# Down's first Strassen product on fp16 parts with a scale of its own

## The chip, the cores and the metric

The kernel runs on one core of a Trainium2 chip, as one program. The metric is the device time of one execution in microseconds; a kernel is measured by the median over several runs. Names of engines in this text: TensorE (PE in the profile, its weight loads PEld), VectorE (DVE), ScalarE (ACT), GpSimd (POOL) and SyncE (SP, which here only issues DMAs).

## The reference

An encoder of two layers on one sequence of 1024 tokens with 1024 channels. Each layer mixes tokens by attention and by a convolution module, adds the result to the residual stream x, and then applies a gated feed-forward block, which the change concerns:

```python
for l in range(DEPTH):                      # DEPTH = 2
    h = _rmsnorm(x, g_mix[l])
    ...                                     # attention heads and convolution module
    x = x + y
    h2 = _rmsnorm(x, g_ffn[l])
    z = _dwconv(h2 @ w_up[l], w_dw_ffn[l], b_dw_ffn[l])       # 1024 -> 2 * 2816, kernel of 3
    zg, zv = jnp.split(z, 2, axis=-1)
    x = x + (jax.nn.silu(zg) * zv) @ w_down[l]                # 2816 -> 1024
return _rmsnorm(x, g_final)
```

Everything is float32 in the reference. The kernel has to come close to float32, so it splits each operand of a matmul into a high part and a low part and adds three products: high by high, high by low, low by high.

## The kernel before

A layer runs through projections, attention, the output product with the heads and the convolutions, then Up (`h2 @ w_up`) and Down (the product with `w_down`). The work around the change is laid out by `feed`: a list of steps, each with some matmuls, and for each step a list of other work with a rank. `put(step, rank, f)` files a piece of work, and `feed` walks through the steps, emits the step's matmuls and then the filed work in order of rank. So the order of instructions on each engine is fixed by hand; engines run through their own queues in order and wait for each other by semaphores. All DMAs of this part are issued by SP, except those that add in memory, which POOL issues.

**Up** (`up_steps`). The 2816 channels are 22 blocks f of 128 (NF = 22), for the gate half and the value half. Each block is a 2 by 2 product of halves (tokens, and columns of the weight), made with seven Strassen products i in the order 1, 2, 6, 5, 7, 3, 4 (`UP_ORDER`). One product is one step: 4 tiles of the contraction by 3 part products, 12 matmuls of 128x512. Weights are cast to fp16 parts with a power of two as scale, which comes from the sum of squares of the block's weights: `own_squares` adds them up per partition, `own_total` sums over partitions with a matmul against ones, and `own_scale` makes the exponent from it with small instructions on VectorE. For block f these stand 14 and 12 steps ahead of the block's first product (`UP`), so those of the last block, f = 21, stand in the steps of block 19. `evict` takes products out of PSUM with the scale undone; some products add up in the same bank, and an eviction must come between. After its taps and its gate, a block of activations is squared and added up into a column of `self.ds` (`act_squares`, columns 0 to 21), and so are the rows of `w_down` (`sum_squares`, columns 22 to 43). Activations are stored to memory, except the last four blocks (KEPT = 18), which stay.

**Down** (`down_steps`). The 22 blocks are the contraction. They are cut into two halves of 11, the tokens into two halves of 512 (`done`, `rest`) and the columns of the weight into two halves of 512, and again seven Strassen products are made, in the order 1, 5, 6, 3, 7, 2, 4 (`ORDER`). A step is one product and one channel tile j of 11: four column tiles m by three part products, 12 matmuls. Four PSUM banks hold a product's sum; products 1, 6, 7 and 4 add up in bank set 0, and 5, 3 and 2 in bank set 1 (`BANK_SET`). Before a step of its own, product i needs

- `fetch(i, j)`, 8 steps ahead, even j: two channel tiles of the weight by DMA, into the three buffers `wr`;
- `turn(i, j)`, 4 steps ahead: the weight's parts, into the eight buffers `ws`;
- `combine(i, j)`, 3 steps ahead: the sum or difference of activations;
- `pair(i, j)`, 2 steps ahead: the activations' parts.

Products other than 1 use fp16 parts. Their scales come from all columns of `self.ds`: `total` and `scales` run after step 6 of product 1, since the last activations are only then squared. Product 1 starts before that, and it takes the parts without a scale, in the type fp32r, by the helper `pair` at L1749 (a cast on ScalarE at L1752, a difference on VectorE at L1754). When it is done, `evict(1, m)` adds it to x as it is (L1573), and `rescale(m)` multiplies its bank by the scales of the others, so that product 6 can add to it (L1517). Products of the others are evicted with L1456, their parts made at L1493 and L1494 (weights, two channel tiles at a time) and L1540 and L1541 (activations). The matmuls of all are at L1551, those of Up at L1306; `total` is at L1500, `own_total` at L1246.

In attention, `sums` writes the reciprocals of the softmax sums of a head into a tile `rs`, and a DMA stores that tile to memory (L1904 to L1906).

Of the kernel before, what the change touches and what calls it, by code (L numbers as in the profile page):

```python
# [9 lines left out]
F32 = mybir.dt.float32  # L10
F32R = mybir.dt.float32r
I32 = mybir.dt.int32
F16 = mybir.dt.float16
BF16 = mybir.dt.bfloat16
AF = mybir.ActivationFunctionType
ALU = mybir.AluOpType
AX = mybir.AxisListType
# [15 lines left out]
NF = DFF // 128  # L33
# [65 lines left out]
LEFT = 4  # L99
# [22 lines left out]
BANK_SET = {1: 0, 6: 0, 7: 0, 4: 0, 5: 1, 3: 1, 2: 1}  # L122
# [22 lines left out]
class Encoder:  # L145
# [787 lines left out]
    def scales(self, l, f):  # L933
        nc = self.nc
        ps = self.bank(f"sc{l}p", (128, 9))
        nc.tensor.matmul(ps, self.ones, f[:, 0:9], start=True, stop=True)
        col = lambda i: f[:, i:i + 1]
        nc.vector.tensor_copy(out=f[:, 0:9], in_=ps)
        nc.vector.tensor_tensor(out=col(13), in0=col(0), in1=col(1), op=ALU.add)
        self.half_exponent(col(17), col(13))  # L940
        self.power(col(21), col(17), -1.0, 200.0)
        self.power(col(22), col(17), 1.0, 39.0)
        return col(21), col(22)
# [233 lines left out]
    def up_steps(self, l, steps, put):  # L1177
        nc, a = self.nc, self.a
# [1 line left out]
        seq = START + [(i, f) for f in range(LEFT, NF) for i in UP_ORDER if (i, f) not in START]  # L1180
        base = len(steps)
        at = {p: base + q for q, p in enumerate(seq)}
        self.kept = {}
        raw, wts, zs, st, sums, scale, back, nback = defaultdict(dict), {}, defaultdict(dict), {}, {}, {}, {}, {}
        self.ds = self.cp.tile([128, 2 * NF], F32, name=f"ds{l}", tag="ds", bufs=1)
        sub = lambda o, p, q, op=ALU.subtract: nc.vector.tensor_tensor(out=o, in0=p, in1=q, op=op)
# [27 lines left out]
        def scales(ps, out, w):  # L1214
            ps = ps.rearrange("p (f e) -> p f e", e=2)
            scale, back, nback, v, h = (out[:, i * w:(i + 1) * w] for i in range(5))
            nc.vector.tensor_reduce(out=v, in_=ps, op=ALU.add, axis=AX.X)
            self.half_exponent(h, v)
            self.power(scale, h, -1.0, 204.0)
            for o, at in ((back, self.back), (nback, self.nback)):  # L1220
                nc.vector.tensor_scalar(out=o.bitcast(I32), in0=h.bitcast(I32), scalar1=EXPONENT, scalar2=at, op0=ALU.mult, op1=ALU.add)
            return scale, back, nback
# [19 lines left out]
                squares(f, e, st["sums", f][:, 6:7].bitcast(BF16)[:, e:e + 1])  # L1242

        def own_total(f):
            st["total", f] = self.pp.tile([128, 2], F32, name=f"wt{l}_{f}", tag=f"d{6 + (f > LEFT and (f + 1) % 2)}", bufs=1)
            nc.tensor.matmul(st["total", f], self.ones_b, st["sums", f][:, 6:7].bitcast(BF16), start=True, stop=True)  # L1246

        def own_scale(f):
            scale[f], back[f], nback[f] = scales(st.pop(("total", f)), st.pop(("sums", f)), 1)

        PAIRS = {1: (1, 2), 2: (1, 2), 5: (5, 6), 6: (5, 6), 3: (3, 7), 7: (3, 7), 4: (4,)}

# [141 lines left out]
        for f in range(LEFT):  # L1394
            at_step((13, 13, 15, 15)[f], 6 + f, sum5, f)
            for i, ms in LEFT_AT.items():
                m, g = ms[f], f % 2
# [4 lines left out]
        for q, (i, f) in enumerate(seq):  # L1402
            n = base + q
            steps.append(lambda i=i, f=f: product(i, f))
            m = EVICT.get((i, f), n + 1)
            put(int(m), m % 1 * 10, lambda i=i, f=f: evict(i, f))
        for f in range(LEFT, NF):
            n = m = at[1, f]
# [16 lines left out]
        for f in range(NF):  # L1425
            n = max(at[2, f], at[3, f], at[6, f]) + 1
            n = n if f >= LEFT else TAPS_AT[0][f]
# [4 lines left out]
            m = max(at[7, f], at[4, f]) + 2 if f >= LEFT else TAPS_AT[1][f]  # L1432
# [8 lines left out]
        for j in range(NF // 2):  # L1441
            n = at[1, 7 + j * 13 // 11]
# [7 lines left out]
    def down_steps(self, l, steps, put):  # L1450
        nc, a = self.nc, self.a
        base, last, half = len(steps), l == DEPTH - 1, NF // 2
        done, rest = HALVES
        act, x, casts, w, pairs, ps, nxt, sq, late_r, turns, st = {}, {}, {}, {}, {}, {}, {}, {}, {}, {}, {}
        sub = lambda o, p, q, op=ALU.subtract: nc.vector.tensor_tensor(out=o, in0=p, in1=q, op=op)  # L1455
        plus = lambda o, p, by: nc.vector.scalar_tensor_tensor(out=o, in0=p, scalar=by, in1=o, op0=ALU.mult, op1=ALU.add)  # L1456
# [27 lines left out]

        def turn(i, j):
            raw = casts[i, j - j % 2]
            if i == 1:
                t = self.pair(raw[:, j % 2], f"wd{l}_{i}{j}", "ws")
                w[i, j] = t[:, 0], t[:, 1]
            elif j % 2 == 0:  # L1490
                n = min(2, half - j)
                t = self.tmp("ws", f"wd{l}_{i}{j}", F16, (128, 2, 2, 512))
                nc.scalar.activation(out=t[:, 0:n, 0], in_=raw, func=AF.Copy, scale=st["w"])  # L1493
                nc.vector.scalar_tensor_tensor(out=t[:, 0:n, 1], in0=raw, scalar=st["w"], in1=t[:, 0:n, 0], op0=ALU.mult, op1=ALU.subtract)  # L1494
                for k in range(n):
                    w[i, j + k] = t[:, k, 0], t[:, k, 1]

# [16 lines left out]

        def rescale(m):
            p = ps[BANK_SET[1], m]
            nc.vector.tensor_scalar(out=p, in0=p, scalar1=st["up"], scalar2=None, op0=ALU.mult)  # L1517

        def combine(i, j):
            p, q = act[j], act.get(half + j)  # L1520
# [11 lines left out]
        def pair(i, j):  # L1532
            src = {1: (j, rest), 5: (j, rest), 6: (j, rest), 3: (half + j, done), 7: (j, done), 2: (half + j, rest),
                   4: (half + j, rest)}[i]
            name, tag, raw = f"ab{l}_{i}{j}", "b" if i == 4 else "m", act[src[0]][:, src[1]]
            if i == 1:
                pairs[i, j] = self.pair(raw, name, tag)
            else:
                t = pairs[i, j] = self.tmp(tag, name, F16, (128, 2, 512))
                nc.scalar.activation(out=t[:, 0], in_=raw, func=AF.Copy, scale=st["a"])  # L1540
                nc.vector.scalar_tensor_tensor(out=t[:, 1], in0=raw, scalar=st["a"], in1=t[:, 0], op0=ALU.mult, op1=ALU.subtract)  # L1541
            if i == 4:
                act.pop(half + j)

# [24 lines left out]
        def evict(i, m):  # L1569
            o, cs = {1: (0, rest), 5: (4, done), 6: (0, done), 3: (0, done), 7: (4, done), 2: (0, rest), 4: (4, rest)}[i]  # L1570
            xm = x[o + m][:, cs]
            if i == 1:
                sub(xm, xm, ps[BANK_SET[i], m], ALU.add)  # L1573
            else:
                plus(xm, ps[BANK_SET[i], m], st["nback" if o else "back"])

# [5 lines left out]
        for i, j in order:  # L1582
            n = at[i, j]
# [5 lines left out]
            else:  # L1589
                m = j - tail  # L1590
# [13 lines left out]
        for m in range(4):  # L1604
            put(at[1, half - 1] + 2 + m // 2, 2, lambda m=m: rescale(m))
# [5 lines left out]
        for i in ORDER[:-1]:  # L1611
            for m in range(4):
                put(at[i, half - 1] + 1, 1, lambda i=i, m=m: evict(i, m))
        n5 = at[4, tail]
        for m in range(4):
            if not last:
                put(n5 + m + (m < 3), 1, lambda m=m: evict(4, m))
                continue
            for c in range(2):
                n = n5 + 4 * c + m  # L1620
                put(n + 1 - c, 1 + c, lambda c=c, m=m: evict_end(c, m))
                if m < 3 - c:
                    put(n + 1, 2.5 if c else 2.6, lambda c=c, m=m: gather_end(c, m))
# [8 lines left out]
        sums = lambda c, ks, cs=None: self.norm_sums(l + 1, x, nxt, c, ks, cs)  # L1632
# [148 lines left out]
    def attention(self, l, u, conv, away, spill, kvs, loaded, ahead, wo, begun):  # L1781
        nc = self.nc
# [118 lines left out]
        def sums(h, main, st, y, rb):  # L1901
            pr = self.bank(f"sr{l}_{h}", (8, 128))
            nc.tensor.transpose(pr, st["sums"], self.ident)
            rs = self.cp.tile([8, 128], F32, name=f"rs{l}_{h}", tag="rs", bufs=2)  # L1904
            nc.vector.reciprocal(out=rs, in_=pr)
            nc.sync.dma_start(out=sd[h].rearrange("(a b) -> a b", a=8), in_=rs)  # L1906
            nc.sync.dma_start(out=rb[main, :], in_=sd[h:h + 1].partition_broadcast(64))
            if h == HEADS - 2:
                for c, cs in enumerate(HALVES):
                    agenda[LAST_MULT[c]].append(lambda cs=cs: nc.vector.scalar_tensor_tensor(out=y[main, cs], in0=y[main, cs], scalar=1.0, in1=rb[main, cs], op0=ALU.mult, op1=ALU.mult))  # L1910
            elif h % 2:
                agenda[h * 8 + 10 + Y_DELAY].append(lambda: nc.gpsimd.tensor_tensor(out=y, in0=y, in1=rb, op=ALU.mult))
                agenda[h * 8 + 10 + Y_DELAY + (Y_SPLIT if h < 5 else Y_LAST)].append(
                    lambda: ys.append(self.split(y, f"ys{l}_{h}", on_pool=True)))
# [30 lines left out]
        total = HEADS * 8  # L1945
        agenda = defaultdict(list)
        late, rest = [], {j: list(away[j]) for j in range(4)}
        while any(rest.values()):
            j = max((j for j in rest if rest[j]), key=lambda j: (all(j != e for e, _ in late[-2:]), len(rest[j]), -j))
# [3 lines left out]
        for i, (j, t) in enumerate(late):  # L1953
            n = LATE_FROM + max(int((SIDE_TIME - LATE_FROM) * sum(costs[:i]) / sum(costs)), kinds[i] != "act")
# [31 lines left out]
        for n in range(-2, total + 2):  # L1986
# [13 lines left out]
            if n + 2 < total:  # L2000
                h, qt = divmod(n + 2, 8)
# [202 lines left out]
```

## Time and profile before

| | |
|---|---|
| median of 3 runs | 2181.2 us (2181.03 to 2181.38) |
| profiled execution | span 2179.0 us, 29766 instructions |
| around the span, from the median | 2.2 us |
| busy PE / DVE / ACT / POOL | 2169.7 / 1844.7 / 1456.6 / 537.2 us |
| mean granted clock of TensorE | 0.999 |
| Down's product 1, first layer, by its matmuls' records | 884.85 to 915.25 us |
| the same, second layer | 1965.64 to 1996.05 us |

The span runs from the first to the last instruction of the profiled execution; its time as the runs count it is not listed beside it, so the 2.2 us are the median's excess over this span. Busy time is that in which an engine has an instruction of the program under way. Matmuls overlap, so the duration of one is longer than the distance from one to the next; how fast TensorE goes is read from the distance, that is from many matmuls in a stretch. In the rows of groups, two numbers stand after the count: busy time in us and the mean of one in ns. In the rows by line, three durations in ns are the least, the median and the longest.

### The profile page before, as it was taken

The numbers are of one execution on the slowest core, as the hardware profiler recorded it, in microseconds if no ns is written. First come the engines' busy times: TensorE is split into PE (matmuls) and PEld (weight loads), VectorE is DVE, ScalarE is ACT, GpSimd is POOL, SyncE is SP. The second block draws the span as 40 slices with busy tenths as digits, with TensorE's granted clock in tenths as the row PEclk, the third lists the DMA queues.
The fourth block names the chain that finished last, engine by engine and source line by source line (L and its number), as shares of the span: only waits on it lengthen the run. The fifth ranks groups of instructions, "written<-read, shape, count | busy, mean of one in ns | idle before, by whom it ended". The sixth has DMA issues, their size and how long they took to land.

```text
span 2179.0 us, 29766 instructions
## 1 busy us (share of the span) xinstructions
PE 2169.7 (100%) x10722; PEld 1260.7 (58%) x10722; DVE 1844.7 (85%) x2531; ACT 1456.6 (67%) x2183; POOL 537.2 (25%) x534
## 2 busy tenths in 40 slices
PE   9999999999999999999999999999999999999998
PEld 8887665754444444644488876667544444446445
DVE  6989999879998887887859789998898888878877
ACT  6455888746898886554623668886478888865544
POOL 1223777211111111000012355771112111110000
PEclk9999999999999999999999999999999999999999
DMA  6898878754688885554578986886646888856533
GB/s 195 184 187 212 164 152 171 245 163 104 149 244 259 222 261 145 193 178 151 166 177 164 188 207 134 159 186 200 175 100 164 261 241 242 241 141 218 182 111 122
DMA packets 163013, 400.96 MB, mean 184 GB/s; under 512 B 21888, under 2 KB 29936, under 8 KB 162864
## 3 DMA queue, kind: packets, MB, share of 16 engines
q0 software_dynamic: 62528, 145.89, 36.4%
q1 hardware_dynamic: 100048, 252.63, 33.8%
q8 instruction: 84, 1.38, 0.3%
q10 hardware_dynamic: 288, 0.53, 0.1%
q14 instruction: 65, 0.53, 0.1%
HBM read 270.75 MB, written 69.66 MB: 156 GB/s over the span
## 4 chain that ended last, share of the span: by engine, by line
PE 98%; ACT 1%; DVE 1%; issue 0%; DMA 0%; DVEq 0%; ACTq 0%
PE p L1306 36%; PE pd L1551 18%; PE po L1026 7%; PE s L1818 7%; PE t L1858 5%; PE pq L245 3%; PE pa L245 3%; PE o L1880 2%; PE pkv L245 2%; PE pg L245 2%; PE pg L564 2%; PE pn L245 2%; PE o L1885 1%; PE pv L1794 1%; PE pk L245 1%; PE pa L564 1%
## 5 line engine op out<-in xcount | busy, mean ns | idle before, releaser
L1306 PE MATMUL p<-b,w 128*128 128x512 f16 x3696 | 800.0, 379 | 0.2
L1306 PEld LDWEIGHTS <-w 128*128 128x128 f16 x3696 | 358.7, 98 | 431.9 <-issue 0.8
L1551 PE MATMUL pd<-ab,wd 128*128 128x512 f16 (+2 forms) x1920 | 404.2, 373 | 0.0
L1196 POOL DMA_DIRECT2D wu<-in_w_up x176 | 152.2, 879 | 770.2 <-DVE w L1270 581.5
L1551 PEld LDWEIGHTS <-wd 128*128 128x128 f16 x1656 | 161.9, 98 | 179.4 <-issue 0.5
L1818 PE MATMUL s<-k,q 96*128 96x512 f16 x768 | 186.9, 379 | 0.0
L1270 DVE SCALAR_TENSOR_TENSOR w<-wu,wf,w 128x512 f16<-128x512 f32 (+1 forms) x216 | 177.2, 834 | 3.6 <-ACT w L1267 3.6
L1861 DVE SCALAR_TENSOR_TENSOR pt<-t,pt 128x512 f16<-128x512 f32 x256 | 163.0, 676 | 10.0 <-ACT pt L1860 9.0
L1267 ACT ACTIVATE w<-wu,wf 128x512 f16<-128x512 f32 (+1 forms) x216 | 164.8, 781 | 0.1
L1860 ACT ACTIVATE pt<-t 128x512 f16<-128x512 f32 x256 | 139.1, 596 | 32.0 <-PE t L1858 30.0
L1820 DVE TENSOR_REDUCE mx<-s 128x1 f32<-128x1024 f32 x128 | 155.0, 1211 | 1.0 <-PE s L1818 1.0
L1540 ACT ACTIVATE ab<-ac,ds 128x512 f16<-128x512 f32 x108 | 75.5, 717 | 108.7 <-DVE ac L1455 73.0
L1828 ACT ACTIVATE p<-s,mx 128x1024 f32<-128x1024 f32 x128 | 143.3, 1120 | 2.2 <-DVE mx L1820 1.8
L2039 DVE SCALAR_TENSOR_TENSOR conv<-gate,par,conv 128x1009 f32<-128x1009 f32 (+14 forms) x110 | 139.9, 1274 | 3.1 <-ACT conv L659 0.4
L2056 POOL TENSOR_SCALAR late<-gate,par 128x1019 f32<-128x1019 f32 (+13 forms) x99 | 135.5, 1368 | 27.2 <-PE pn L245 13.9
L1858 PE MATMUL t<-ident,p 128*128 128x128 f32 x1024 | 136.6, 275 | 0.9 <-ACT p L1828 0.6
L1858 PEld LDWEIGHTS t<-ident,p 128*128 128x128 f32 x1024 | 116.8, 141 | 34.8 <-issue 7.4
L1766 DVE SCALAR_TENSOR_TENSOR o<-zg,par,o 128x1023 f32<-128x1023 f32 x88 | 112.7, 1281 | 8.9 <-ACT o L1760 7.4
L1314 DVE SCALAR_TENSOR_TENSOR zg<-p,wf,zg 128x512 f32<-128x512 f32 x72 | 54.0, 750 | 71.2 <-PE p L1306 61.6
L1766 DVE SCALAR_TENSOR_TENSOR v<-zv,par,v 128x1023 f32<-128x1023 f32 x88 | 112.1, 1276 | 0.0
L1818 PEld LDWEIGHTS <-q 96*128 96x128 f16 x768 | 74.0, 97 | 64.6 <-issue 2.1
L1541 DVE SCALAR_TENSOR_TENSOR ab<-ac,ds,ab 128x512 f16<-128x512 f32 x108 | 79.9, 748 | 19.2 <-ACT ab L1540 19.2
(2179 smaller groups left out, 3814.1 us busy)
## 6 DMA issues: line engine op xcount, KB each, us to landing
wu<-in_w_up SPq DMA_DIRECT2D x98, 512.0 KB
wu<-in_w_up POOLq DMA_DIRECT2D x176, 256.0 KB, 4.8
sd<-in_w_down SPq DMA_DIRECT2D x44, 512.0 KB
ws<-sd SPq DMA_DIRECT2D x44, 512.0 KB
act<-v SPq DMA_DIRECT2D x36, 512.0 KB
ac<-act SPq DMA_DIRECT2D x72, 256.0 KB
wo<-in_w_o POOLq DMA_DIRECT2D x32, 256.0 KB, 7.7
x_mix<-y SPq DMA_DIRECT2D x32, 256.0 KB
```

Of the source, the lines that this page charges most:

```text
L245: nc.tensor.matmul(ps[:, HALVES[c]], w, x[:, HALVES[c]], start=(k == 0 and s == 0), stop=(k == n - 1 and s == 2))
L1026: self.nc.tensor.matmul(ps, p[:, sl], q[:, cs], start=(k == 0 and t == 0), stop=(k == 3 and t == 2))
L1196: nc.gpsimd.dma_start(out=dst, in_=src, accum_op=ALU.add)
L1267: nc.scalar.activation(out=t, in_=src, func=AF.Copy, scale=scale[f])
L1270: nc.vector.scalar_tensor_tensor(out=t, in0=src, scalar=scale[f], in1=hi, op0=ALU.mult, op1=ALU.subtract)
L1306: nc.tensor.matmul(ps, w[p][:, k * 128:(k + 1) * 128], b[:, q], start=(i in (1, 5, 2) and k == 0 and t == 0), stop=(k == 3 and t == 2), sk ...
L1551: nc.tensor.matmul(ps[t, m][:, cs], w[i, j][p][:, m * 128:(m + 1) * 128], b[:, q, cs], start=(i in (1, 5, 2) and j == 0 and s == 0), stop= ...
L1766: self.nc.vector.scalar_tensor_tensor(out=o[:, a:b], in0=z[:, at + a:at + b], scalar=self.par[l][:, tap:tap + 1], in1=o[:, a:b], op0=ALU.m ...
L1818: nc.tensor.matmul(ps[:, cs], q[0:96, i, qs], k[0:96, j, cs], start=(s == 0), stop=(s == 2))
L1820: nc.vector.tensor_reduce(out=mx, in_=ps, op=ALU.max, axis=AX.X, negate=True)
L1858: nc.tensor.transpose(tp[:, i, qi * 128:(qi + 1) * 128], st["p"][2 * qp + qi][:, kt * 128:(kt + 1) * 128], self.ident)
L1861: nc.vector.scalar_tensor_tensor(out=lo, in0=tp, scalar=P_SCALE, in1=hi, op0=ALU.mult, op1=ALU.subtract)
```

## The change

Product 1 of Down is made on fp16 parts like the other six. Its scales are ready before Down starts: `own_total` of Up's last block gets a second matmul, which sums those columns of `ds` over partitions that belong to the first half of the channels (activation blocks 0 to 10 and weight rows 0 to 10, 22 columns), and `own_scale` makes from them a scale for the activations, one for the weights and their inverse, in a new small tile `dw`. `turn`, `pair` and `evict` lose their special case for product 1 and use these scales; `rescale` multiplies by the inverse too. So that the new tile has room, `rs` in attention gets one buffer in place of two. The helper `pair` is not called by these functions any more.

```diff
         def own_total(f):
-            st["total", f] = self.pp.tile([128, 2], F32, ...)
-            nc.tensor.matmul(st["total", f], self.ones_b, st["sums", f][:, 6:7].bitcast(BF16), start=True, stop=True)
+            n = 2 + NF * (f == NF - 1)
+            st["total", f] = self.pp.tile([128, n], F32, ...)
+            nc.tensor.matmul(st["total", f][:, 0:2], self.ones_b, st["sums", f][:, 6:7].bitcast(BF16), start=True, stop=True)
+            if f == NF - 1:
+                half = self.ds[:, 0:2 * NF].rearrange("p (e h f) -> p e h f", e=2, h=2)[:, :, 0]
+                nc.tensor.matmul(st["total", f][:, 2:n], self.ones, half, start=True, stop=True)
 
         def own_scale(f):
-            scale[f], back[f], nback[f] = scales(st.pop(("total", f)), st.pop(("sums", f)), 1)
+            ps = st.pop(("total", f))
+            scale[f], back[f], nback[f] = scales(ps[:, 0:2], st.pop(("sums", f)), 1)
+            if f == NF - 1:
+                t = self.cp.tile([128, 8], F32, name=f"dw{l}", tag="dw", bufs=1)
+                nc.vector.tensor_reduce(out=t[:, 0:2], in_=ps[:, 2:2 + NF].rearrange("p (e f) -> p e f", e=2), op=ALU.add, axis=AX.X)
+                nc.vector.tensor_scalar(out=t[:, 0:2], in0=t[:, 0:2], scalar1=2.0 ** -60, scalar2=None, op0=ALU.max)
+                self.half_exponent(t[:, 2:4], t[:, 0:2])
+                self.power(t[:, 4:6], t[:, 2:4], -1.0, 204.0)
+                self.power(t[:, 6:8], t[:, 2:4], 1.0, 50.0)
+                nc.vector.tensor_tensor(out=t[:, 6:7], in0=t[:, 6:7], in1=t[:, 7:8], op=ALU.mult)
+                self.opened.update(a=t[:, 4:5], w=t[:, 5:6], back=t[:, 6:7])
...
         def turn(i, j):
             raw = casts[i, j - j % 2]
-            if i == 1:
-                t = self.pair(raw[:, j % 2], f"wd{l}_{i}{j}", "ws")
-                w[i, j] = t[:, 0], t[:, 1]
-            elif j % 2 == 0:
-                n = min(2, half - j)
+            if j % 2 == 0:
+                n, by = min(2, half - j), self.opened["w"] if i == 1 else st["w"]
                 t = self.tmp("ws", f"wd{l}_{i}{j}", F16, (128, 2, 2, 512))
-                nc.scalar.activation(out=t[:, 0:n, 0], in_=raw, func=AF.Copy, scale=st["w"])
-                nc.vector.scalar_tensor_tensor(out=t[:, 0:n, 1], in0=raw, scalar=st["w"], in1=t[:, 0:n, 0], op0=ALU.mult, op1=ALU.subtract)
+                nc.scalar.activation(out=t[:, 0:n, 0], in_=raw, func=AF.Copy, scale=by)
+                nc.vector.scalar_tensor_tensor(out=t[:, 0:n, 1], in0=raw, scalar=by, in1=t[:, 0:n, 0], op0=ALU.mult, op1=ALU.subtract)
...
         def rescale(m):
             p = ps[BANK_SET[1], m]
-            nc.vector.tensor_scalar(out=p, in0=p, scalar1=st["up"], scalar2=None, op0=ALU.mult)
+            nc.vector.tensor_scalar(out=p, in0=p, scalar1=st["up"], scalar2=self.opened["back"], op0=ALU.mult, op1=ALU.mult)
...
         def pair(i, j):
...
-            if i == 1:
-                pairs[i, j] = self.pair(raw, name, tag)
-            else:
-                t = pairs[i, j] = self.tmp(tag, name, F16, (128, 2, 512))
-                nc.scalar.activation(out=t[:, 0], in_=raw, func=AF.Copy, scale=st["a"])
-                nc.vector.scalar_tensor_tensor(out=t[:, 1], in0=raw, scalar=st["a"], in1=t[:, 0], op0=ALU.mult, op1=ALU.subtract)
+            by = self.opened["a"] if i == 1 else st["a"]
+            t = pairs[i, j] = self.tmp(tag, name, F16, (128, 2, 512))
+            nc.scalar.activation(out=t[:, 0], in_=raw, func=AF.Copy, scale=by)
+            nc.vector.scalar_tensor_tensor(out=t[:, 1], in0=raw, scalar=by, in1=t[:, 0], op0=ALU.mult, op1=ALU.subtract)
...
         def evict(i, m):
...
             if i == 1:
-                sub(xm, xm, ps[BANK_SET[i], m], ALU.add)
+                plus(xm, ps[BANK_SET[i], m], self.opened["back"])
...
         def sums(h, main, st, y, rb):
...
-            rs = self.cp.tile([8, 128], F32, name=f"rs{l}_{h}", tag="rs", bufs=2)
+            rs = self.cp.tile([8, 128], F32, name=f"rs{l}_{h}", tag="rs", bufs=1)
```

More of the change, by code (lines that the diff above doesn't have):

```diff
@@ L1182, in up_steps @@
         at = {p: base + q for q, p in enumerate(seq)}
-        self.kept = {}
+        self.kept, self.opened = {}, {}
         raw, wts, zs, st, sums, scale, back, nback = defaultdict(dict), {}, defaultdict(dict), {}, {}, {}, {}, {}
@@ L1244, in own_total @@
         def own_total(f):
-            st["total", f] = self.pp.tile([128, 2], F32, name=f"wt{l}_{f}", tag=f"d{6 + (f > LEFT and (f + 1) % 2)}", bufs=1)
-            nc.tensor.matmul(st["total", f], self.ones_b, st["sums", f][:, 6:7].bitcast(BF16), start=True, stop=True)
-        def own_scale(f):
-            scale[f], back[f], nback[f] = scales(st.pop(("total", f)), st.pop(("sums", f)), 1)
+            n = 2 + NF * (f == NF - 1)
+            st["total", f] = self.pp.tile([128, n], F32, name=f"wt{l}_{f}", tag=f"d{6 + (f > LEFT and (f + 1) % 2)}", bufs=1)
+            nc.tensor.matmul(st["total", f][:, 0:2], self.ones_b, st["sums", f][:, 6:7].bitcast(BF16), start=True, stop=True)
+            if f == NF - 1:
+                half = self.ds[:, 0:2 * NF].rearrange("p (e h f) -> p e h f", e=2, h=2)[:, :, 0]
+                nc.tensor.matmul(st["total", f][:, 2:n], self.ones, half, start=True, stop=True)
+        def own_scale(f):
+            ps = st.pop(("total", f))
[9 more added lines that the diff above has]
+                self.opened.update(a=t[:, 4:5], w=t[:, 5:6], back=t[:, 6:7])
         PAIRS = {1: (1, 2), 2: (1, 2), 5: (5, 6), 6: (5, 6), 3: (3, 7), 7: (3, 7), 4: (4,)}
```

## The prediction

> **What bounds the kernel now.** I read the page first (engines, slices, chain), then the chain of waits in order of time around the two places that the change touches, then the groups by form, and last the timelines of TensorE, VectorE and ScalarE there.
>
> ```profile
> span 2179.0 us, 29766 instructions
> ...
> PE 2169.7 (100%) x10722; PEld 1260.7 (58%) x10722; DVE 1844.7 (85%) x2531; ACT 1456.6 (67%) x2183; POOL 537.2 (25%) x534
> ...
> PEclk9999999999999999999999999999999999999999
> ...
> PE 98%; ACT 1%; DVE 1%; issue 0%; DMA 0%; DVEq 0%; ACTq 0%
> ```
>
> TensorE is busy for 2169.7 of 2179.0 us at full granted clock, and the chain that ended last lies on it for 98%. Only what changes TensorE's own stream, or what makes it wait, can move the end. The chain around the change (start, length, what, how many instructions), in the first layer, and its one row for the second that matters:
>
> ```profile
> 838.55 0.00 PE wt L1246
> 838.56 46.64 PE p L1306 x216
> 885.20 19.06 PE pd L1551 x84
> 904.26 0.15 PE ds0p L1500 x2
> 904.41 158.65 PE pd L1551 x732
> ...
> 1965.99 19.07 PE pd L1551 x84
> ```
>
> The first 84 and the next 48 matmuls of L1551 are Down's product 1 (11 channel tiles, 4 column tiles, 3 part products: 132). They run at 19.06/84 = 226.9 ns each; the last 216 of Up, on fp16 parts with the same 128x512 moving tile, at 46.64/216 = 215.9 ns. No gap stands between the pieces. The rows by form say which is which:
>
> ```profile
> L1551 PE MATMUL pd<-ab,wd 128*128 128x512 f16 x1512 | 327.3, 379 | 0.0
> ...
> L1551 PE MATMUL pd<-ab,wd 128*128 128x512 f32 x264 | 61.1, 392 | 0.0
> ```
>
> 264 = 2 layers of 132. The means (379, 392) are durations of overlapping instructions; the spacing is in the chain.
>
> **The change, part by part.**
>
> *1. Product 1's matmuls become fp16.* At the spacing of Up's row, 84 take 18.14 us where 19.06 stands: 0.92 less. The piece of 732 holds 48 of product 1 and 684 fp16 ones: 732 at 215.9 ns would be 158.06, so the 48 cost 0.59 more than fp16 ones would (at the 11 ns of the 84 it would be 0.53). Together 1.45 to 1.51 us a layer; I take 1.48, for two layers 2.96 us, all of it on the path. Below this nothing comes unless fp16 pieces in this stage run slower than in Up; 684 of them already stand in the same piece.
>
> *2. One more matmul with fp32 ones, 22 columns, behind the last own total of Up (L1246).* It appears as two instructions, as the 44-column ds0p does (0.15 us on the chain). A nearer case is L1228, eight columns of fp32 between fp16 matmuls:
>
> ```profile
> 441.75 0.12 PE wt L1228 x2
> ...
> L1228 PEld LDWEIGHTS wt<-wa,ones_r x4: 190/190/190, 441.4 to 1522.4; 128*128 128x128 f32 x4
> ```
>
> That bounds it below at 0.12. Here it follows the two-column total, whose piece on the chain is 0.00, so it has no long matmul to load its first weights behind; above, I take both loads of 190 ns bare, 0.38. The first load can still begin while the total's predecessor runs out, so I take 0.2 a layer: 0.4 in all. The two ends are 0.24 and 0.76.
>
> *3. Six small VectorE instructions (reduce, maximum, exponent, two powers, product) in the last own scale.* The same six stand in Down's scales:
>
> ```profile
> 904.45 0.20 DVE L1505 TENSOR_REDUCE ds<-ds0p 128x2 f32<-128x44 f32 x1 [4.18 <-PE ds0p L1500]
> 904.69 0.17 DVE L1506 TENSOR_SCALAR ds<-ds 128x2 f32<-128x2 f32 x1
> ...
> 905.38 0.15 DVE L1511 TENSOR_TENSOR ds<-ds 128x1 f32<-128x1 f32 x1
> ...
> 905.64 0.69 DVE L1754 TENSOR_TENSOR ab<-ac,ab 128x512 fp32r<-128x512 f32 x1
> ```
>
> From 904.45 to 905.38 is 0.93 us. Queued behind them on VectorE are filter taps, a weight part and the zv eviction that TensorE's next product on that bank needs:
>
> ```profile
> 843.87 0.75 DVE L1314 SCALAR_TENSOR_TENSOR zv<-p,wf,zv 128x512 f32<-128x512 f32 x1 [0.86 <-PE p L1306]
> ```
>
> VectorE idles 0.86 us before that eviction, so it comes at most 0.07 late; the product that adds on the bank is a whole product away (12 x 0.216 = 2.59 us, less 0.75 for the eviction). Cost: nothing. The matmul of part 2 waits for the squares in ds that it reads; the last of them are written before block 18 starts, and it stands nine steps of 12 matmuls later, so this costs nothing either.
>
> *4. The casts of weights and activations change form.* Rows of the old and of the new form (the new one is already used by the other six products):
>
> ```profile
> L1752 ACT CAST ab<-ac x22: 602/607/621, 879.6 to 1987.2; 128x512 fp32r<-128x512 f32 x22
> L1754 DVE TENSOR_TENSOR ab<-ac,ab x22: 681/686/694, 880.7 to 1989.4; 128x512 fp32r<-128x512 f32 x22
> L1752 ACT CAST wd<-wd_10r x4: 608/609/611, 875.5 to 1958.8; 128x512 fp32r<-128x512 f32 x4
> ...
> L1493 ACT ACTIVATE wd<-wd_52r,ds x2: 1133/1134/1136, 910.7 to 1991.5; 128x1024 f16<-128x1024 f32 x2
> L1494 DVE SCALAR_TENSOR_TENSOR wd<-wd_52r,ds,wd x2: 1278/1280/1281, 912.1 to 1992.9; 128x1024 f16<-128x1024 f32 x2
> ...
> L1540 ACT ACTIVATE ab<-ac,ds x108: 704/721/725, 910.0 to 2138.4; 128x512 f16<-128x512 f32 x108
> L1541 DVE SCALAR_TENSOR_TENSOR ab<-ac,ds,ab x108: 741/747/755, 910.8 to 2149.0; 128x512 f16<-128x512 f32 x108
> ...
> L1456 DVE SCALAR_TENSOR_TENSOR x<-pd,ds,x x52: 473/743/752, 943.3 to 2169.5; 128x512 f32<-128x512 f32 x44, 128x256 f32<-128x256 f32 x8
> L1455 DVE TENSOR_TENSOR x<-x,pd x8: 681/684/686, 914.5 to 1997.1; 128x512 f32<-128x512 f32 x8
> L1517 DVE TENSOR_SCALAR pd<-pd,ds x8: 754/758/761, 919.4 to 2003.4; 128x512 f32<-128x512 f32 x8
> ```
>
> Activations: 11 x (721 - 607) = 1.25 us more ScalarE and 11 x 61 ns = 0.67 us more VectorE a layer. Weights: eleven pairs of about 0.61 and 0.69 become five of 1.13 and 1.28 and one single (0.71, 0.75): ScalarE 6.7 to 6.4, VectorE 7.5 to 7.15. Eviction of product 1 becomes the form of the others (L1455 0.684 to L1456 0.743, four a layer, 0.24 us), and the rescale keeps its operation and gets a second scalar (L1517, 0.758 now; bounds 0 and 0.06, as for the evictions, four a layer). VectorE's sum in the stage grows by about 0.6 us. Whether TensorE sees that depends on three margins.
>
> *Opening.* Both halves of a weight pair are now cast at the even step, one step early for the odd one.
>
> ```profile
> 883.43 1.24 ACT L1760 ACTIVATE o<-zg,par 128x1024 f32<-128x1024 f32 x1 [2.66 <-DVE zg L1314]
> ...
> 885.22 0.69 DVE L1754 TENSOR_TENSOR ab<-ac,ab 128x512 fp32r<-128x512 f32 x1 [1.82 <-ACT ab L1752]
> ```
>
> Activation tile 1 is ready at 885.91; TensorE starts on it at 885.20 + 12 x 0.216 = 887.79 after the change. The cast is 0.11 + 0.06 longer, and the weight pair ahead of it adds up to 0.6 on VectorE, of which the idle times shown (2.66, 1.82) take most. At worst 886.7: 1.1 us to spare. Tiles 2 to 7 have more.
>
> *Around Down's total.* VectorE waits 4.18 us for ds0p, then makes tile 8 of the activations, ready at 905.64 + 0.69 = 906.33. TensorE starts it 12 matmuls after 904.41: 907.13 before; after the change 907.00, against 906.39. It uses the low part in its second matmul: 0.8 us of cover, the thinnest of all. With that gone, each 0.1 us late costs 0.1 us a layer.
>
> *After product 1.* TensorE comes 0.5 us earlier from the total on:
>
> ```profile
> 920.69 0.75 DVE L1541 SCALAR_TENSOR_TENSOR ab<-ac,ds,ab 128x512 f16<-128x512 f32 x1
> ```
>
> This is tile 3 of product 5, ready at 921.44. TensorE uses it at 904.41 + 48 x 0.228 + 36 x 0.216 = 923.13, after the change 922.55; VectorE's surplus since the total is 4 x 0.06 for casts and 0.24 for evictions, at most 0.12 for rescales, so 922.0: 0.5 us left, and the low part is not needed until one matmul later. No wait.
>
> *5. The queues and buffers.* SP's fetch of a later weight pair waits for VectorE to have read an older one; that read now ends one step sooner, so loads are issued up to 2.6 us earlier, at a DMA share of 0.46 in the first part of this stage:
>
> ```profile
> SPq L1482 <- DVE wd L1754: 43.7, 12, 6.1
> ...
> 884.85:904.10 19.25, 19.25 (x87) 15.93 (x86) 14.53 (x19) 12.57 (x22) 0.00 (x0) 1.00 0.46 146
> ```
>
> POOL issues nothing here. Six slots of the weight buffer are taken in place of eleven, so slot waits can only shrink. In attention the reciprocal tile rs has one buffer in place of two: a head's reciprocal waits for the store of the head before.
>
> ```profile
> L1905 DVE RECIPROCAL rs<-sr x14: 931/933/935, 245.2 to 1454.2; 8x128 f32<-8x128 f32 x14
> ...
> SPq L1907 <- DMA sd<-rs: 30.8, 14, 3.8
> ...
> 361.75 0.94 DVE L1905 RECIPROCAL rs<-sr 8x128 f32<-8x128 f32 x1
> ...
> 373.40 0.94 DVE L1905 RECIPROCAL rs<-sr 8x128 f32<-8x128 f32 x1
> ```
>
> The store lands within 3.8 us, while the closest two stand 11.6 us apart (361.75 and 373.40). Cost: nothing.
>
> *Sum.* -2.96 + 0.4 = -2.56 us against the profiled span of 2179.0, that is 2176.4. The median of the runs is 2181.2, 2.2 us more than this span, for what lies around it: 2178.6. With the ends of parts 1 and 2: 2178.2 to 2179.1.
>
> **A rule weighed against the rows.** The weight load takes 190 ns for fp32 and 98 for fp16:
>
> ```profile
> L1551 PEld LDWEIGHTS <-wd x1656: 95/98/181, 915.2 to 2169.1; 128*128 128x128 f16 x184
> L1551 PEld LDWEIGHTS pd<-ab,wd x264: 187/188/192, 884.8 to 1995.6; 128*128 128x128 f32 x132
> ```
>
> If that load were in the open, 264 x 90 ns = 23.8 us would go and the time would be 2157.8. The spacing differs by 11 ns only, so it is hidden behind the matmul before. The Trainium skill, "TensorE: Matmul & The Clock Gate", section "Weight-path perf modes — Fast Weight Load (FWL) and DoubleRow", says that 128 non-fp32 weights load about twice as fast and fp32 gains nothing; the two rows agree. The same page's "Back-to-back issue gap" gives 512/2.4 + 2.5 = 215.8 ns a matmul with no term for the type: the fp16 rows agree; the 226.9 does not, and by that rule the saving would be zero.
>
> **The rivals.**
> - *Nothing is saved* (0.06): the 227 ns come from this stage (its banks, its reads) and not from the type. For it: the 48 behind the total are not quite as the 84. Against: 684 fp16 matmuls into the same banks at 215.9. Time: 2181.2 + 0.4 = 2181.6.
> - *The other side: TensorE waits for VectorE in the opening* (0.07). In-order double casts of 1.28 us stand ahead of the activation casts. It begins to cost once tile 1 is more than 1.9 us late (887.79 less 885.91), and the kernel is slower than before once it is 1.9 + 1.28 = 3.2 us late, twice. Two more double casts and an eviction ahead of it (1.28 + 1.28 + 0.75 = 3.3) would do that: 2181.4; a third cast gives 2183.9, and 0.2% slower needs 5.4 us. Against: the idle times above.
> - *A thin margin fails by a little* (0.10): tile 8 or product 5's tile 3 comes up to 1 us late; up to 2 us are given back: 2178.6 to 2180.6.
> - *The weight load is in the open* (0.02): 2157.8.
> - *My forecast* (0.75): 2178.6.
>
> **How the numbers follow.** A measurement of this kernel tells about 0.2% from no change, 4.4 us: 2176.8 to 2185.6. The forecast lies within it, as do the first and third rivals and most of the second. The range for 8 in 10 takes in the forecast and the third rival, with half a microsecond below for a spacing better than Up's: 2177.6 to 2180.8. Faster by over 0.2% gets 0.05 (open load, and a forecast wrong by two thirds), slower 0.04, the same 0.91.
>
> **What the changed profile would show.** On the chain 84 matmuls of L1551 at 18.14 us, not 19.06, and no f32 form there; a new piece of 0.1 to 0.4 us behind the last own total; no idle time or stretched spacing at tile 1, tile 8 or product 5; VectorE still idle some 4 us before ds0p. Wrong would be: spacing still 227, a wait of TensorE for an ab tile, or a piece of waiting on the chain in Up's last four blocks.

## The result and the profile after

The changed kernel takes 2178.45 us (median of 21 runs, 2177.97 to 2179.8), the kernel before 2181.38 us in the runs beside it (21 runs, 2180.82 to 2182.24): ratio 0.9986, 95% interval 0.998 to 0.9993. That is 2.93 us less, or 0.13%, where 2.56 was the sum of the prediction.

The page of the changed kernel: span, engines, and the share of engines in the chain that ended last.

```profile
span 2177.3 us, 29765 instructions
...
PE 2167.7 (100%) x10726; PEld 1237.7 (57%) x10726; DVE 1848.6 (85%) x2533; ACT 1459.4 (67%) x2173; POOL 537.1 (25%) x534
...
PE 96%; ACT 1%; DMA 1%; DVE 1%; issue 0%; SPq 0%; DVEq 0%; ACTq 0%
```

All of Down's matmuls of 512 columns are now one form, the 264 that were f32 among them (1512 + 264 = 1776):

```profile
L1560 PE MATMUL pd<-ab,wd 128*128 128x512 f16 x1776 | 384.6, 379 | 0.0
```

TensorE has 2.0 us less of work, VectorE 3.9 and ScalarE 2.8 us more, and TensorE is still what ends the kernel. The chain in order of time (start, length, what, count) around the change, first layer and second; L1247 is the own total, L1250 the new matmul, L1320 Up, L1560 Down, L1511 Down's total:

```profile
839.50 0.00 PE wt L1247
839.50 0.24 PE wt L1250 x2
839.74 46.62 PE p L1320 x216
886.37 18.13 PE pd L1560 x84
904.50 0.15 PE ds0p L1511 x2
904.65 157.99 PE pd L1560 x732
...
1918.91 0.00 PE wt L1247
1918.91 0.24 PE wt L1250 x2
1919.15 46.62 PE p L1320 x216
1965.78 18.13 PE pd L1560 x84
1983.91 0.15 PE ds1p L1511 x2
1984.06 157.99 PE pd L1560 x732
```

A layer's account is read here piece by piece: 19.06 to 18.13 (-0.93), 158.65 to 157.99 (-0.66), the new piece (+0.24), Up's 216 (-0.02): -1.37 us, -2.74 in two layers. A second way, which needs no pieces, is the distance from the last own total of the first layer to that of the second. Before, the second stood here:

```profile
1919.34 0.00 PE wt L1246
```

1919.34 - 838.55 = 1080.79 before, 1918.91 - 839.50 = 1079.41 after: 1.38 us less. The two agree. The profiled span fell by only 1.7 us, since this execution reached the first own total 0.95 us later than the one before (839.50 against 838.55), ahead of everything that the change does in Down. That is the scatter of single executions and not the change: of the kernels below that have the changed code up to there, e6 and e7 have 838.51 and 838.53, e4 and e8 839.19 and 839.22, and e5, with the code of before, has 839.23. In the execution of the changed kernel the chain went through a load:

```profile
11.01 13.51 DMA x<-in_x
```

The chain of the execution of before has no such piece, but a late start does not need one (that of e5 has none either). The distance between the layers is free of it and is used for all kernels below.

### The profile page after: what moved, and what is told of

The parts are those of the page before. It is cut to its first block, busy times and chain, and to the rows that moved or that the text cites. A ratio compares the mean times of both kernels' runs of the same rounds, so it can differ in the third digit from the quotient of the medians.

```text
span 2177.3 us, 29765 instructions
## 1 busy us (share of the span) xinstructions
PE 2167.7 (100%) x10726; PEld 1237.7 (57%) x10726; DVE 1848.6 (85%) x2533; ACT 1459.4 (67%) x2173; POOL 537.1 (25%) x534
## 3 DMA queue, kind: packets, MB, share of 16 engines
q8 instruction: 84, 1.38, 0.3%
## 4 chain that ended last, share of the span: by engine, by line
PE 96%; ACT 1%; DMA 1%; DVE 1%; issue 0%; SPq 0%; DVEq 0%; ACTq 0%
PE p L1320 36%; PE pd L1560 18%; PE po L1026 7%; PE s L1827 7%; PE t L1867 5%; PE pq L245 3%; PE pa L245 3%; PE o L1889 2%; PE pkv L245 2%; PE pg L245 2%; PE pn L245 2%; PE o L1894 1%; PE pv L1803 1%; PE pg L564 1%; PE pk L245 1%; DMA x<-in_x 1%
## 5 line engine op out<-in xcount | busy, mean ns | idle before, releaser
L1320 PE MATMUL p<-b,w 128*128 128x512 f16 x3696 | 800.3, 379 | 0.3
L1320 PEld LDWEIGHTS <-w 128*128 128x128 f16 x3696 | 358.8, 98 | 431.7 <-issue 0.8
L1560 PE MATMUL pd<-ab,wd 128*128 128x512 f16 (+1 forms) x1920 | 400.6, 371 | 0.0
L1560 PEld LDWEIGHTS <-wd 128*128 128x128 f16 x1920 | 187.9, 98 | 209.9
```

The lines of the kernel that those rows point to most:

```text
L1320: nc.tensor.matmul(ps, w[p][:, k * 128:(k + 1) * 128], b[:, q], start=(i in (1, 5, 2) and k == 0 and t == 0), stop=(k == 3 and t == 2), sk ...
L1560: nc.tensor.matmul(ps[t, m][:, cs], w[i, j][p][:, m * 128:(m + 1) * 128], b[:, q, cs], start=(i in (1, 5, 2) and j == 0 and s == 0), stop= ...
```

## The experiments

**e1: the price without the gain.** The functions `own_total` and `own_scale` of the changed kernel, the tile `dw` and the single buffer for `rs`, put into the kernel before; nothing uses the new scales.

```diff
-    nc.tensor.matmul(st["total", f], self.ones_b, ...)
+    nc.tensor.matmul(st["total", f][:, 0:2], self.ones_b, ...)
+    nc.tensor.matmul(st["total", f][:, 2:n], self.ones, half, ...)      # f == NF - 1
+    ...                                                                 # six instructions on VectorE
```

> The kernel before with only the new total added: the 22-column matmul, the six small VectorE instructions, the tile dw and one buffer for rs; product 1 stays on fp32r parts and the new scales are not used. My theory: two instructions of TensorE cost 0.24 us a layer on the chain (as in the changed kernel), the VectorE instructions, the tile and the single buffer cost nothing: 2181.4 + 0.5 = 2181.9 us, product 1 still 19.06 us for 84 matmuls. Rival (VectorE's 0.93 us delays an eviction in Up's last blocks): over 1 us more, above 2182.4, with a piece of waiting on the chain behind block 19.

Measured: 2181.49 us against 2181.3, ratio 1.0002 (0.9992 to 1.0011). The chain:

```profile
838.82 0.00 PE wt L1247
838.83 0.24 PE wt L1250 x2
...
885.69 19.05 PE pd L1565 x84
...
1919.74 0.00 PE wt L1247
```

The piece is 0.24 us as in the changed kernel, and product 1 takes as long as before. TensorE's chain runs on without a wait, so VectorE's six instructions delay nothing. Layer to layer 1080.92, 0.13 more than before, where the pieces (0.24 for the pair, some 0.04 less in the others) give 0.20; to about 0.1 us is what such a distance can tell. The time's interval cannot tell 0.5 us from none.

**e2: the fp32 total ahead of the bf16 one.** In the changed kernel, the two matmuls of `own_total` change places.

> The changed kernel with the 22-column fp32 total ahead of the two-column bf16 total of the same block, not behind it. If the 0.24 us come from the first fp32 weight load that has no long matmul to hide behind, the piece falls to the 0.12 to 0.15 us of the other fp32 pairs, 0.1 us a layer, 2178.2 us. Rival (the pair costs what its 22 columns cost, wherever it stands): 0.24 us stays, 2178.4 us.

```profile
839.00 0.13 PE wt L1249 x2
839.13 0.01 PE wt L1250
...
1918.25 0.13 PE wt L1249 x2
```

0.24 becomes 0.14 with the bf16 total. The columns are the same, so it is the place that counts, and the reading that the first fp32 weight load now hides behind a matmul of 512 columns fits; the rival, that the columns set the price, falls. 2178.18 us (ratio to before 0.9986, 0.9977 to 0.9995), layer to layer 1079.25, which is 0.16 less than the changed kernel.

**e3: one buffer for `rs` in the kernel before.** The edit is `bufs=2` to `bufs=1`, nothing else.

> The kernel before with one buffer for rs in place of two, nothing else. My theory: no wait, 2181.4 us within 0.1%, the reciprocals start 11.6 us apart at the least as before. Rival (the single buffer or the shifted addresses of all later tiles cost or bring time): a difference over 0.3 us between the layers' starts of attention and of its end in the trace.

2181.28 us, ratio 1.0001 (0.9992 to 1.001).

```profile
838.65 0.00 PE wt L1246
...
1919.43 0.00 PE wt L1246
```

Layer to layer 1080.78 against 1080.79. To within the 0.1 us of such a distance, the single buffer costs nothing, and neither do the shifted addresses of the tiles behind it.

**e4: product 2 on fp32r in the changed kernel.** The special case that product 1 lost, given to product 2.

```diff
 def turn(i, j):
+    if i == 2:
+        t = self.pair(raw[:, j % 2], f"wd{l}_{i}{j}", "ws")
+        w[i, j] = t[:, 0], t[:, 1]
...
 def pair(i, j):
+    if i == 2:
+        pairs[i, j] = self.pair(raw, name, tag)
...
 def evict(i, m):
+    if i == 2:
+        sub(xm, xm, ps[BANK_SET[i], m], ALU.add)
```

> The changed kernel with Down's product 2 on fp32r parts without a scale, as product 1 was before; it starts a fresh sum in the other bank set. If the 11 ns a matmul belong to the type, 132 matmuls of product 2 now stand 227 ns apart and the kernel takes 1.48 us more a layer, 2181.4 us. Rival (the 11 ns belonged to the opening of Down, its banks or reads): product 2 stays at 216 ns and the time at 2178.4 us.

2181.28 us, ratio to before 1.0 (0.9991 to 1.0009): the gain is gone.

```profile
839.19 0.00 PE wt L1247
...
886.05 18.13 PE pd L1566 x84
904.18 0.15 PE ds0p L1514 x2
904.34 159.47 PE pd L1566 x732
...
1920.08 0.00 PE wt L1247
```

Product 1 keeps its 18.13, and the piece that holds product 2 grows from 157.99 to 159.47: 1.48 us for 132 matmuls, 11.2 ns each, in another place and into the other bank set. Layer to layer 1080.89, 1.48 more than the changed kernel. So the surplus belongs to the type, and the rival that it belonged to this stage falls. The profile of before already spoke against that rival, at a place where the prediction did not look: the projections, far from Down, are on fp32r parts too, and their 48 matmuls of 512 columns take 10.88/48 = 226.7 ns each.

```profile
40.01 10.88 PE pa L245 x48
```

Which operand's type makes the surplus, that of the weights or that of the moving tile, is not told apart by any run here.

**e5 and e10: what the 11 ns consist of.** In the kernel before, each fp32r matmul of product 1 is cut into two of 256 columns (e5) or four of 128 (e10), each with its own weight load.

```diff
-nc.tensor.matmul(ps[t, m][:, cs], w[i, j][p]..., b[:, q, cs], ...)
+for q4 in ((slice(0, 256), slice(256, 512)) if i == 1 else (cs,)):       # e10: four of 128
+    nc.tensor.matmul(ps[t, m][:, q4], w[i, j][p]..., b[:, q, q4], ...)
```

> The kernel before with each fp32r matmul of product 1 cut into two of 256 columns, 264 a layer, each with its own weight load of 188 ns. If the columns set the 227 ns and the load is hidden behind them, a half one takes no less than the load: about 190 ns, 50 us for product 1 in place of 30, 40 us more in two layers (2221 us). Rival (the load with what follows it sets 227 ns whatever the columns): 60 us for product 1, 60 us more (2241 us). Second rival (loads overlap fully, also behind a short matmul): 114 ns, no change of time.

2184.85 us against 2181.39, one time each. My theory (2221 us) was wrong; of the three forecasts the last, called the second rival, was nearly right. The chain of e5 has

```profile
839.23 0.00 PE wt L1246
...
885.87 20.14 PE pd L1552 x168
...
906.16 159.22 PE pd L1552 x780
```

168 in 20.14 us are 119.9 ns each, though one load takes 192 ns. By their records, loads thus overlap one another, and not only the matmul ahead. 226.9 for 512 columns and 119.9 for 256 give 107.0 for 256 columns (0.418 ns a column) and 12.9 left over for each matmul. The fp16 matmuls have the same price a column: 215.9 at 512 and, by the single records at the end of Down, 109.1 at 256 differ by 106.8 (0.417 ns a column), with 2.3 left over. The 11 ns are thus a fixed surplus of an fp32r matmul, as far as two sizes show it.

> The kernel before with each fp32r matmul of product 1 cut into four of 128 columns, 528 a layer. Cut into two, the distance was 120 ns (20.14 us for 168), whole it is 227: a fixed 13 ns beside 0.418 ns a column. My theory (a fixed surplus for each matmul of this type, whatever its columns): 66 to 67 ns, 336 of them in 22.4 us on the chain up to Down's total, about 5 us a layer more than before, 2191 us. Rival (weight loads of 190 ns overlap only two deep): 95 ns, 336 in 31.9 us, 20 us a layer more, 2221 us.

2241.01 us against 2181.27, one time each, and neither my theory's 2191 nor the rival's 2221:

```profile
887.39 37.47 PE pd L1552 x336
...
L1552 PEld LDWEIGHTS pd<-ab,wd 128*128 128x128 f32 x1056 | 118.4, 192 | 0.3
```

37.47/336 = 111.5 ns a matmul of 128 columns, where 66 were forecast. The weight loads follow each other without a gap, one each 111.5 ns. That the columns do not set this distance is shown by the profile of before, where eight fp32 matmuls of one column take 0.89/8 = 111 ns each:

```profile
2170.30 0.89 PE rx_768p L275 x8
```

So the likeliest bound is the load, one for each matmul, which the matmul of 256 columns (119.9) just covers and that of 512 by far. Some other floor of a matmul of this type is not excluded, and the fixed 12.9 ns could not be put to a third size here.

**e6, e7, e8: how thin the cover is.** Idle instructions of VectorE are put at three places of the changed kernel, a maximum of a tile with itself:

```diff
+def idle():
+    k = self.kept[19][:, rest]                       # e8: kept[18]
+    for _ in range(2):                               # e8: 8
+        sub(k, k, k, ALU.max)
+put(base + 6, 2.9, idle)                             # e7: base + 12, 2.5; e8: base - 1, 2.9
```

For e6 and e7 they are two, in a step of product 1 and of product 5; for e8 eight, in the last step of Up. Each has one time. The cover is the start of the second matmul of a tile (the first that uses the low part) less the end of that tile's cast, by the single records.

> The changed kernel with two idle VectorE instructions of 0.61 us each (a maximum of a tile with itself) ahead of the cast of activation tile 8 of product 1, behind Down's scales. In the changed kernel that tile's low part is ready 0.66 us before TensorE uses it. My theory: of 1.22 us, 0.56 come out as a wait of TensorE at tile 8, in each layer: 1.1 us more than the changed kernel, 2179.5 us. Rival (there is more cover than the records show): no stretched distance at tile 8.

2179.79 us. The chain leaves TensorE where it waits and runs through the cast of tile 8:

```profile
906.20 0.75 DVE ab L1550
...
907.00 155.58 PE pd L1560 x719
```

TensorE's distance there is 917 ns where 216 is usual, 0.70 us of wait; two more of 0.13 and 0.12 come at tiles 3 and 4 of product 5. Together 0.95 us a layer (0.85 by the distance from layer to layer), more than the 0.56 expected. An idle instruction takes 0.72 us from start to start and not 0.61; both work on one tile, so that the second seems to wait for the first. And the lateness is carried on to product 5, which I had thought VectorE would make up.

> The changed kernel with the same two idle VectorE instructions behind the first two rescales, ahead of tile 3 of product 5, which has 0.53 us of cover, tile 4 behind it 0.41. My theory: 0.7 us of wait at tile 3 and 0.1 at tile 4, 0.8 us a layer, 2180.1 us. Rival (VectorE catches up): no stretched distance there.

2179.95 us. The distances at tiles 3 and 4 of product 5 are 1063 and 330 ns: 0.85 and 0.11 us of wait, 0.96 a layer (0.92 by the distance from layer to layer) where 0.8 was expected.

> The changed kernel with eight idle VectorE instructions (4.9 us) in the last step of Up, ahead of the cast of activation tile 1 of product 1. VectorE has 1.92 us of idle time there and the tile 1.20 us of cover. My theory: 4.9 - 1.9 - 1.2 = 1.8 us of wait at tile 1, and 0.5 at the tiles behind it at the most, since the queue behind is full: 2 us a layer, 2182.4 us, which would be slower than before. Rival (the opening has more cover): no wait up to 4.9 us, 2178.4 us.

2183.7 us, above the kernel before (2181.39 beside it). VectorE's cast of tile 1 in the changed kernel:

```profile
887.05 0.75 DVE L1550 SCALAR_TENSOR_TENSOR ab<-ac,dw,ab 128x512 f16<-128x512 f32 x1 [1.92 <-ACT ab L1549]
```

The timeline of VectorE in e8, and behind it the chain:

```profile
884.77 5.76 DVE L1469 TENSOR_TENSOR v<-v 128x512 f32<-128x512 f32 x8
890.46 0.74 DVE L1550 SCALAR_TENSOR_TENSOR ab<-ac,dw,ab 128x512 f16<-128x512 f32 x1
...
890.46 0.75 DVE ab L1550
891.21 0.04 issue
891.25 15.48 PE pd L1560 x71
```

The eight take 5.76 us; 5.76 - 1.92 - 1.20 = 2.64, and TensorE's distance at tile 1 is 2739 ns, 2.52 of wait, with none behind it (cover 0.78 and 0.32 at tiles 2 and 3). So the cover read from the records holds to about 0.1 us, and a delay here that is large enough makes the kernel slower than the one before: layer to layer e8 has 1081.91, 1.12 more than before.

**e9: both totals on bf16.** The squares are added up in bf16, and the new total and Down's total become one bf16 matmul each.

```diff
+self.db = self.ds[:, 0:NF].bitcast(BF16)
-nc.scalar.activation(..., func=AF.Square, accum_out=self.ds[:, f:f + 1])
+nc.scalar.activation(..., func=AF.Square, accum_out=self.db[:, f:f + 1])
-nc.tensor.matmul(st["ps"], self.ones, self.ds[:, 0:2 * NF], ...)
+nc.tensor.matmul(st["ps"], self.ones_b, self.db, ...)                    # and own_total's alike
-f = self.ds[:, 0:16]
+f = self.ds[:, NF:NF + 16]
```

> The changed kernel with the sums of squares of activations and of w_down's rows kept in bf16, so that the 22-column total and Down's 44-column total are one bf16 matmul each against bf16 ones, as the own totals of Up. If the fp32 pairs cost 0.24 and 0.15 us a layer on the chain and a bf16 total 0.00 to 0.03, the kernel is 0.7 us faster than the changed one: 2177.8 us. Rival (the small matmul itself is not what costs, but the change of type in the stream): the pieces stay at 0.1 us or more, 2178.2 us.

2177.6 us (2177.32 to 2178.25, 11 runs), ratio to before 0.9984 (0.9975 to 0.9993); the kernel before had 2181.34 beside it.

```profile
839.15 0.00 PE wt L1248
839.15 0.04 PE wt L1251
...
903.95 0.02 PE ds0p L1514
...
1918.17 0.01 PE wt L1248
```

0.24 and 0.15 us become 0.04 and 0.02, and the layer distance 1079.02, 0.39 less than the changed kernel's (0.33 by these two pieces). The rival, that the change of type in the stream costs 0.1 us whatever the matmul, falls. This is the fastest of the kernels by its chain and by its median; by the times alone its interval overlaps that of the changed kernel.

## Why the prediction was right, step by step

**The spacing (part 1)** carried the sum and held: 18.13 us measured for 18.14. The 48 behind the total saved 0.66 where 0.59 was the upper value, so the term is 1.59 us a layer and not 1.48. The 0.07 come from the 732, which now stand 157.99/732 = 215.8 ns apart and not 215.9 as in Up. Why the 48 had cost more than 11 ns each shows in the records of before: right behind the total one distance is 314 ns and most of the next nine are 230 to 236, before they settle at 227. Two sizes off, -3.18 for -2.96 here and +0.48 for +0.4 below, make most of the difference between the 2.56 us predicted and the 2.74 by the chain. The remaining 0.2 to the medians' 2.93 lies well inside the interval of the ratio. e4 shows that the type is the cause. The rival that nothing is saved is out.

That 2178.6 us was forecast and 2178.45 measured is closer than the saving itself, by luck: the three runs it started from lay 0.2 us lower than the 21 beside the result. The lower end of the prediction's sum was added up wrong, too: its own ends give 2179.0 - 3.02 + 0.24 + 2.2 = 2178.4 and not 2178.2.

**The added pair (part 2)** cost 0.24 where 0.2 was taken between 0.12 and 0.38. The reason given fits: e2 takes 0.1 away by putting the pair behind a long matmul. The upper end, two loads bare at 190 ns, was too high: e10 shows fp32 loads each 111.5 ns, and two of these are 0.22.

**VectorE's six instructions (part 3)** took as long as their rows of before (840.87 to 841.83, 0.96 us for 0.93) and cost nothing:

```profile
840.87 0.17 DVE L1257 TENSOR_REDUCE dw<-wt 128x2 f32<-128x22 f32 x1
...
841.83 1.28 DVE L1775 SCALAR_TENSOR_TENSOR v<-zv,par,v 128x1023 f32<-128x1023 f32 x1
...
845.03 0.75 DVE L1328 SCALAR_TENSOR_TENSOR zv<-p,wf,zv 128x512 f32<-128x512 f32 x1
```

The zv eviction comes 5.53 us after the own total, before 843.87 - 838.55 = 5.32; less the 0.24 of the new matmuls it is on time, and its idle time of 0.86 us is used up, as counted.

**The cover (part 4)** was right in that TensorE waits nowhere in this stage, and its sizes were too large. By the records the cover is 1.20 us at tile 1 (predicted 1.1 up to the first matmul, 1.3 up to the second), 0.66 at tile 8 (0.8), 0.53 at tile 3 of product 5 (0.5 up to the first matmul, 0.7 up to the second), and 0.41 at its tile 4, which the prediction did not look at. It called tile 8 the thinnest of all, but it had counted tile 8 up to the second matmul and tile 3 only up to the first; counted alike, tile 3 was already the thinner one. At tile 8 and tile 3 VectorE was ready when the prediction said, to 0.1 us; TensorE came sooner. The prediction took the start of a piece of the chain, here 904.65 us, for the start of its first matmul, which by its record is 904.47, 0.18 us ahead.

The rescale, for which 0 to 0.06 us were left open, took the upper end, as the working for tile 3 had assumed:

```profile
L1528 DVE TENSOR_SCALAR pd<-pd,ds,dw x8: 814/818/825, 920.1 to 2002.9; 128x512 f32<-128x512 f32 x8
```

Two of them stand ahead of tile 3 of product 5 and two more ahead of its tile 4. One of the signs left a part out. VectorE was to be idle some 4 us before Down's total, and its wait fell from 4.18 to 3.34 us:

```profile
904.68 0.20 DVE L1516 TENSOR_REDUCE ds<-ds0p 128x2 f32<-128x44 f32 x1 [3.34 <-PE ds0p L1511]
```

That is not VectorE's extra work: counted from the chain's start of product 1, VectorE begins this wait at 15.07 us before (904.45 - 4.18 - 885.20) and at 14.97 after (904.68 - 3.34 - 886.37). The total comes 0.93 us sooner, by the gain of the 84 matmuls, and the wait ends with it. VectorE's extra work itself was too small in the prediction, 2 x (0.6 + 0.93) = 3.1 us where the page shows 3.9. Neighbours on VectorE overlap at their ends, so that the old casts stood 0.61 us from the next start (0.69 long) and the new double ones 1.20 (1.28 long). By that distance the weights' casts save VectorE nothing, where the durations promised some 0.35 us a layer.

**The rival on the other side** had tile 1 become 3.2 us later than in the kernel before. The change made it 0.72 us later against the chain's start of product 1 (885.91 - 885.20 = 0.71 before, 887.80 - 886.37 = 1.43 after), where the prediction's worst case was 0.8. e8 added 5.76 - 1.92 = 3.84 to that, which is well above the 3.2, and the kernel did become slower than before. That bears out the cover and the price, but it does not locate the threshold; an estimate from the cover of 1.20 and the gain of 1.38 us a layer is a delay of 2.6 us on top of the changed kernel. The thin-margin rival did not come either, though by the cover of tile 4 some 0.4 us of further work on VectorE in product 5 would have started it.

**The rule on weight loads.** Loads of 190 against 98 ns and their being hidden at 512 columns were read rightly from the rows of before. The Trainium skill, "TensorE: Matmul & The Clock Gate", section "Back-to-back issue gap", gives N/2.4 + 2.5 ns as the gap of a warm matmul, with no term for the type. The rows agree for fp16 (215.9 - 512/2.4 = 2.6 ns) and differ for fp32r (13.6 ns at 512 columns, 13.2 at 256), and the measurement decides.

**e1 and e3** leave nothing that can be seen on the side of the total, the tile and the buffer but the 0.24 us on TensorE.

## What to carry to other kernels

Where one engine is busy without a gap from end to end, count the change of its own stream from the spacing of many instructions in a stretch, not from their durations; here that gave 2.56 of 2.74 us. The other engines' extra work counts only against the time from a tile's readiness to its use. Compute that cover for every tile behind the place of the change, up to the same matmul of each and from the records of single instructions, and not only for the one that looks latest, since a delay in an engine without idle time is carried on to later tiles. Before blaming a stage for a distance, look for the same type in another stage of the same profile. A tiny fp32 matmul in a stream without gaps got cheaper here behind a long matmul (0.24 to 0.13 us) and cheaper still in bf16 (0.04).

## What the runs showed of the hardware

At the full granted clock (1.0), fp32r matmuls stand 226.9 and 119.9 ns apart at 512 and 256 columns, fp16 ones 215.9 and 109.1. Both types pay 0.42 ns a column, so an fp32r matmul has some 13 ns beside its columns and an fp16 one some 2, as far as two sizes show. Fp32 weight loads of 192 ns overlap each other and can follow every 111.5 ns; matmuls of 128 fp32r columns stand just as far apart, and so do fp32 ones of one column (111 ns). Behind an fp32 total, fp32r matmuls took about ten to settle: one of 314 ns, most others 230 to 236, then 227. A VectorE tensor_scalar out of PSUM with two per-partition scalars took 818 ns where one scalar took 758. Two VectorE instructions on the same tile, one after the other, stood 0.72 us apart, where independent ones of the same form stand 0.60 apart.
